# Moving the input sums, the first step tile's weights, the roots and the last chunk's first two tiles of a hybrid encoder layer

## The chip, the cores and the metric

The kernel runs on one core of a Trainium2 chip. The metric is the device time of one execution in microseconds (us). Each profile is one execution, recorded on the chip. The engines are PE (TensorE, matmuls), DVE (VectorE), ACT (ScalarE), POOL (GpSimd) and SP (SyncE, which here issues the loads).

## The reference

```python
def rmsnorm(x, g):
    return x * rsqrt(mean(x * x) + 1e-6) * g
def swiglu(x, wi, wo):
    a, b = split(x @ wi, 2)
    return (silu(a) * b) @ wo          # wi: 1024 x 5632, wo: 2816 x 1024
h = concatenate([meta, x])             # 16 + 512 positions, 1024 channels, fp32
h = h + 0.5 * rmsnorm(swiglu(rmsnorm(h, n[0]), ffn1_wi, ffn1_wo), n[1])
h = h +       rmsnorm(hybrid_mixer(rmsnorm(h, n[2]), ...), n[3])
h = h + 0.5 * rmsnorm(swiglu(rmsnorm(h, n[4]), ffn2_wi, ffn2_wo), n[5])
return h[16:]                          # the 512 positions of x
```

The mixer (a Fourier branch, a gated short convolution and a chunked gated DeltaNet) is not touched by the change.

## The kernel before

Everything is held transposed: channels on partitions (8 blocks of 128, index `k`), positions in the free dimension. `hT` is the residual, `x` the same with the gain of the norm but without its root: the product with `wi` is linear, so the root `rx` of each position is multiplied in afterwards (`scaled`, L531, and the `ev` products L643 and L646). Each fp32 matmul is made of three fp32r products, high by high, high by low and low by high, so that weights and inputs exist as pairs (`wh`, `wl`), (`x` twice), (`gh`, `gl`), (`h`, `l`). A split is a cast on ACT (L229 or L234) and a difference on DVE (L230 or L235). Weights land in `ws` or `wf` by loads on SP's queue and are split into a ring of four `wh` and `wl`.

The sections in order: the first FFN (`ffn`) over all 528 positions in halves of 264 columns; an `edge` (post norm, residual, pre norm and the first three weight units of the next section); the mixer; another `edge`, after which only the 512 real positions are left; the second FFN with matmuls of 512 columns; `finish`, which writes the output. PSUM has four banks `pb` and four `pd`.

Within an FFN there are 22 pairs (a, b) of 128 channels each of `wi`, in `CHUNKS` of 4, 4, 4, 4, 3 and 3. The first four pairs come from plain units: 8 blocks times 3 products into a bank. The other pairs use seven block products instead of eight (Strassen's way in Winograd's form): `seven` builds sums of blocks of the input (the input sums: `h`, `l`, L569 to L582, 128x1056 or 128x1024 elements each; the results are `X`), `one` to `seven` the products. The second product, with `wo`, makes 8 output tiles `m` from each chunk. `second` is one tile, `both` two tiles at once in plain order, `whole` one tile placed as a step between the products; the weights of two tiles come by `double`. For chunk 0 the tiles 0 to 3 come by `both`, and 4 to 7 as step tiles, whose split weights lie in `hx`, a tile in the same room as `hT` (tag "h"). `fetch` loads them. In that room lie the sums' inputs too, so that the room is free when the last sum has been read.

`xstat` sums squares for `rx`: ACT squares, DVE adds into `acc`, and then a step inside a unit (`side`, due at `XF` after the second edge) multiplies by `ones`, so that each partition gets the sum of each position, and `root` (ACT square root, L288, DVE reciprocal, L289) works on 128 partitions by 264 columns. `stat`, used for the post norms, instead sums into one column per 88 or 128 positions, takes the root there (positions on partitions, 88x3), and spreads it by matmuls of `ident` with the root broadcast and a copy (L285). The last chunk's tiles are left to `edge` or `finish` as a tail, in halves of the positions; `part` first copies `y` into the bank (L349), and the matmuls add onto it.

PE runs in the order of the code. The order on the other engines is set by the scheduler of the kernel language from dependencies and priorities: `high_priority(n)` moves what is inside ahead by n (`URGENT` 450, `AHEAD` 150, `AHEAD2` 200). Each engine then works strictly in that order.

Of the kernel before, what the change touches and what calls it, by code (L numbers as in the profile page):

```python
# [28 lines left out]
WARM = 9  # L29
AHEAD = 150  # L30
AHEAD2 = 200
XF = 9.0
URGENT = 450
CHUNKS = (range(0, 4), range(4, 8), range(8, 12), range(12, 16), range(16, 19), range(19, 22))
NU = max(len(c) for c in CHUNKS)
FIRST = 4
# [113 lines left out]
class K:  # L150
# [140 lines left out]
    def xstat(self, C, hT, rx, wait=XW, first=0):  # L291
        V, ACT = self.nc.vector, self.nc.scalar
        W = C.halves[0].stop - C.halves[0].start
        parts = []
        with self.tc.high_priority(first):
            for c in C.halves:
                acc = self.t(self.tp, "acc", [P, HN], F32, 2)[:, :W]
                ACT.activation(acc, hT[:, 0, c], AF.Square)
                for k in range(1, KD):
                    sq = self.t(self.tp, "sx", [P, HN], F32, 2)[:, :W]  # L300
                    ACT.activation(sq, hT[:, k, c], AF.Square)
                    V.tensor_tensor(acc, acc, sq, op=ALU.add)  # L302
                parts.append((acc, rx[:, c]))

        def gen():
            for acc, dst in parts:
                ps = self.dnp()[:, :W]
                self.T.matmul(ps, self.ones, acc, start=True, stop=True)
                self.root(ps, dst)
            yield 0.0  # L310
        self.side(gen(), wait)

# [3 lines left out]
        acc = [self.t(self.tp, "acc", [P, HN], F32, 2)[:, :W] for _ in range(2)]  # L316
        return y, acc

    def evict_y(self, ya, m, ps, gain=None, table=KD - 2, more=False):

        y, acc = ya
        ACT, V = self.nc.scalar, self.nc.vector
        for i, p in ps:
            w = acc[i].shape[1]
            if more:
                V.tensor_tensor(y[i][:, m, :w], y[i][:, m, :w], p, op=ALU.add)
                p = y[i][:, m, :w]
            elif gain is None:
                ACT.copy(y[i][:, m, :w], p)
            else:  # L330
                ACT.activation(y[i][:, m, :w], p, AF.Copy, scale=self.gains[:, gain, m:m + 1])
            if m == 0:
                ACT.activation(acc[i], p, AF.Square)
            else:
                sq = self.t(self.tp, "sy", [P, HN], F32, 1)[:, :w]
                ACT.activation(sq, p, AF.Square)  # L336
                V.tensor_tensor(acc[i], acc[i], sq, op=ALU.add)  # L337
            if more and gain is not None:
                ACT.activation(p, p, AF.Copy, scale=self.gains[:, gain, m:m + 1])
        if m == table:  # L340
            ACT.activation(self.junk, acc[0][:, :1], AF.Sqrt)

# [54 lines left out]
    def edge(self, C, hT, ya, gpost, gpre, tail, switch, nxt, keep=None):  # L397
        nc = self.nc
        V, ACT = nc.vector, nc.scalar
        W = C.halves[0].stop - C.halves[0].start  # L400
        r = self.t(self.tp, "r", [P, L])
        x = (self.xtile(), self.xtile())
        self.rx = rx = self.t(self.tp, "rx", [P, L])

        def step(i, k):
            c = C.halves[i]
            t = self.small()[:, :W]
            V.scalar_tensor_tensor(t, ya[0][i][:, k, :W], self.gains[:, gpost, k:k + 1], r[:, c],  # L408
                                   op0=ALU.mult, op1=ALU.mult)
            V.tensor_tensor(hT[:, k, c], hT[:, k, c], t, op=ALU.add)  # L410
            if keep is not None:
                nc.gpsimd.dma_start(keep[:, k, i * W:(i + 1) * W], hT[:, k, c])
            g = self.gains[:, gpre, k:k + 1]
            ACT.activation(x[0][:, k, c], hT[:, k, c], AF.Copy, scale=g)  # L414
            V.scalar_tensor_tensor(x[1][:, k, c], hT[:, k, c], g, x[0][:, k, c].bitcast(F32),  # L415
                                   op0=ALU.mult, op1=ALU.subtract)

        tiles, tx, tc, more = tail()
        for t in tiles:
            self.evict_y(ya, t[0], [(0, self.part(t, tx, tc[0], W, more and ya[0][0]))], table=tiles[0][0] - 1)  # L420
        post = [self.stat([(ya[1][i], r[:, C.halves[i]])]) for i in range(2)]

        def early():
            for _ in range(5):
                yield
            next(post[0])
            for _ in range(4):
                yield
            next(post[0], None)
            for k in range(3):  # L430
                step(0, k)
        e = early()
        for t in tiles:
            self.evict_y(ya, t[0], [(1, self.part(t, tx, tc[1], W, more and ya[0][1], lambda: next(e, None)))], table=-1)
        for k in range(3, KD):
            step(0, k)
        switch()
        ws = [self.load(a) for a in nxt]
        os = [self.outs(C), self.outs(C), self.outs(C, self.dnp)]
        LAG = 2  # L440
        for i in range(KD + LAG):
            if i in (SB0, SB1):
                next(post[1], None)
            for j in range(3):
                k = i - (LAG if j == 2 else 0)
                if 0 <= k < KD:
                    self.mm(os[j].half[:1], ws[j], x, k, k, k == 0, k == KD - 1)
        for k in range(KD):
            step(1, k)
            for j in range(3):  # L450
                self.mm(os[j].half[1:], ws[j], x, k, k, k == 0, k == KD - 1)
        self.xstat(C, hT, rx, *((XF, URGENT) if keep is not None else ()))
        return x, os

    def finish(self, hT, ya, tail, out):
# [20 lines left out]
        def early():  # L476
# [13 lines left out]
                yield  # L490
            for t in range(2):
                for f in range(2):
                    b = self.big()
                    for i in range(4):
                        T.transpose(b[:, i * P:(i + 1) * P],
                                    hT[:, 4 * f + i, cB.start + t * P:cB.start + (t + 1) * P], ident)
                        if i % 2:
                            yield
                    ACT.copy(hB[:, t, f * 512:(f + 1) * 512], b)
# [116 lines left out]
    def ffn(self, pre, wi, wo, C, hT, gpre, again, gain=None):  # L616
# [40 lines left out]
        with urgent():  # L657
# [1 line left out]
            silu(e[:, 0])  # L659
            self.scaled(e[:, 1], o2)  # L660
            pair(3, e[:, 0, u], e[:, 1, u])
        X, rest = self.seven(hT, C, gpre)
        rest()

        ya = self.start_y(C)
        later = []
# [1 line left out]
        def second(ci, m, w):  # L668

            n = len(CHUNKS[ci])  # L670
            final = ci == len(CHUNKS) - 1
            o = self.outs(C)

            def ks(r):
                for k in r:
                    self.mm(o.full, w, G[ci], (m % 2) * n + k, k, k == 0, k == n - 1)

            def evict():
                ps = [(i, p) for i, (p, _) in enumerate(o.half)]
                with urgent():  # L680
                    if final:
                        return self.evict_y(ya, m, ps, gain, more=True)
                    for i, p in ps:
                        y = ya[0][i][:, m, :W]
                        if ci:
                            V.tensor_tensor(y, y, p, op=ALU.add)  # L686
                        else:
                            ACT.copy(y, p)
            return ks, evict, n
# [13 lines left out]
            ks2([n - 1])  # L703
            evict2()

        for m in range(0, FIRST, 2):
            both(0, m)


# [6 lines left out]

        def fetch(i):
            if i < len(line) and i not in ready:
                ready[i] = double(*line[i], (room[i // 2 % 2], room[2 + i // 2 % 2]))

        def whole():
            nonlocal at
# [73 lines left out]
        for ci in range(1, len(CHUNKS)):  # L796
            n = len(CHUNKS[ci])
            for m in CHUNKS[ci]:
                if m == CHUNKS[ci].start + 1:
                    while at < limit:  # L800
                        whole()
                    acc = 0.0
                    if ci > 1:
                        limit += KD
                rate = (KD if ci > 1 else KD - FIRST) / (2.0 * n)
                nxt = one(m)
                five(nxt)
                slot(rate)
                if st:
                    seven(st)  # L810
                slot(rate)
                two(nxt)
                if st:
                    four(st)
                six(nxt)
                st = nxt
        slot(1.0)
        seven(st)
        while at < limit:
            whole()  # L820
        four(st)
        fin = len(CHUNKS) - 1
        hT = self.htile()
        for k in range(KD):
            nc.sync.dma_start(hT[:, k, u], again[:, k])
        both(fin, 0)

        def tail():
            n = len(CHUNKS[fin])
            ws = [double(fin, m) for m in range(2, KD, 2)]  # L830
            return [(m, [(ws[m // 2 - 1], (m % 2) * n + k, k) for k in range(n)]) for m in range(2, KD)], G[fin], C.halves, True
        return hT, ya, tail


# [756 lines left out]
```

## Time and profile before

| | us |
|---|---|
| median of three runs (lowest to highest) | 1308.08 (1306.58 to 1311.67) |
| the profiled execution, own time | 1309.39 |
| its span | 1307.6 |
| PE busy in the span | 1277.4 |
| first FFN to the first edge, from the span's start | 0 to 369 |
| edge 1 | 369 to 401 |
| mixer | 401 to 925 |
| edge 2 | 925 to 947 |
| second FFN | 947 to 1290 |
| finish | 1290 to 1307.6 |

A matmul's own duration holds its pipeline, so the distance from one start to the next is what it costs in a stream. A number in brackets behind a row of the timeline is how long the engine stood idle before it, and what it waited for. The granted clock in a window is the share of full speed at which PE was allowed to run.

### The profile page before, as it was taken

What the parts mean: (1) busy time and instruction counts of PE and PEld (TensorE: products, weight loads), DVE (VectorE), ACT (ScalarE), POOL (GpSimd) and SP (SyncE); (2) the same over time, 40 slices, a digit from 0 to 9 for tenths busy, and PEclk for the clock granted to TensorE, in tenths of its full rate; (3) what the DMA queues carried; (4) which work ended last, traced back from release to release, by engine and by line L of the source; (5) the groups of instructions that cost most, each with busy time, mean ns of one, the idle gap of its engine ahead of it and who ended that gap; (6) DMA issues with size and microseconds to landing.
All of it is one profiled execution on the core that took longest, in us unless ns stands there. A gap on an engine that the chain in (4) does not pass through costs nothing.

```text
span 1307.6 us, 22834 instructions
## 1 busy us (share of the span) xinstructions
PE 1277.4 (98%) x9001; PEld 1156.1 (88%) x9001; DVE 953.7 (73%) x1878; ACT 609.6 (47%) x1191; POOL 13.5 (1%) x28
## 2 busy tenths in 40 slices
PE   9999999999999999999999999999896999999997
PEld 9999999999989988779977777888875999999996
DVE  7968777766578889568788578463987677777655
ACT  7555444434275642444633444334555554444436
POOL 0000000000000000000000000000200000000000
PEclk9989999999999999999999999999998999999999
DMA  7233223222334222221221212234431332322213
GB/s 255 81 105 106 98 100 102 98 82 73 115 134 162 77 86 85 86 74 66 81 66 49 73 57 89 81 121 146 153 121 65 113 106 98 105 98 93 85 49 129
DMA packets 70205, 129.51 MB, mean 99 GB/s; under 512 B 15820, under 2 KB 24140, under 8 KB 70100
## 3 DMA queue, kind: packets, MB, share of 16 engines
q1 hardware_dynamic: 64244, 124.40, 28.2%
q10 hardware_dynamic: 5088, 1.57, 0.5%
q0 software_dynamic: 768, 2.10, 0.4%
q8 instruction: 70, 1.15, 0.4%
q14 instruction: 35, 0.29, 0.1%
HBM read 120.68 MB, written 7.37 MB: 98 GB/s over the span
## 4 chain that ended last, share of the span: by engine, by line
PE 88%; DVE 7%; ACT 3%; issue 1%; DVEq 0%; ACTq 0%
PE pb L143 55%; PE pd L143 32%; PE pd L147 1%; DVE s L408 1%; DVE x L415 1%; DVE acc L302 1%; DVE h L410 1%; DVE wl L235 1%; DVE wl L230 1%; DVE h L558 0%; ACT wh L229 0%; ACT sy L336 0%; DVE x L235 0%; DVE acc L337 0%; ACT pb L349 0%
## 5 line engine op out<-in xcount | busy, mean ns | idle before, releaser
L143 PE MATMUL pb<-x,wh 128*128 128x264 f32 (+3 forms) x1568 | 356.5, 331 | 5.4 <-ACT x L414 2.5
L143 PEld LDWEIGHTS pb<-x,wh 128*128 128x128 f32 x1568 | 247.7, 190 | 37.7 <-DVE x L415 5.1
L143 PE MATMUL pb<-x,wl 128*128 128x264 f32 (+3 forms) x784 | 219.9, 325 | 0.0
L143 PE MATMUL pb<-gh,h 128*128 128x264 f32 (+1 forms) x816 | 187.7, 327 | 10.6 <-ACT h L229 10.5
L229 ACT CAST wh<-ws 128x1024 fp32r<-128x1024 f32 (+2 forms) x114 | 107.3, 943 | 184.3 <-PE pb L143 145.7
L143 PE MATMUL pd<-x,wh 128*128 128x264 f32 (+2 forms) x1040 | 192.1, 285 | 0.0
L234 ACT CAST wh<-wf 128x1024 fp32r<-128x1024 f32 x108 | 113.4, 1050 | 161.9 <-PE pd L143 126.8
L235 DVE TENSOR_TENSOR wl<-wf,wh 128x1024 fp32r<-128x1024 f32 x108 | 132.0, 1222 | 42.8 <-ACT wh L234 42.7
L143 PEld LDWEIGHTS pd<-x,wh 128*128 128x128 f32 x1040 | 160.5, 189 | 2.0
L143 PEld LDWEIGHTS pb<-gh,h 128*128 128x128 f32 x816 | 131.2, 192 | 23.1 <-ACT h L229 10.9
L230 DVE TENSOR_TENSOR wl<-ws,wh 128x1024 fp32r<-128x1024 f32 (+2 forms) x114 | 123.7, 1086 | 30.7 <-ACT wh L229 30.3
L143 PEld LDWEIGHTS pb<-x,wl 128*128 128x128 f32 x784 | 133.9, 190 | 12.7 <-DVE wl L378 0.2
L143 PE MATMUL pd<-x,wl 128*128 128x264 f32 (+2 forms) x520 | 143.8, 284 | 0.0
L143 PE MATMUL pb<-gl,h 128*128 128x264 f32 (+1 forms) x408 | 110.8, 326 | 0.0
L143 PEld LDWEIGHTS pd<-x,wl 128*128 128x128 f32 x520 | 96.3, 188 | 0.3
L143 PE MATMUL pd<-h,wh 128*128 128x264 f32 (+1 forms) x294 | 82.2, 283 | 0.0
L143 PE MATMUL pd<-l,wh 128*128 128x264 f32 (+1 forms) x288 | 81.7, 284 | 0.0
L143 PE MATMUL pd<-h,wl 128*128 128x264 f32 (+1 forms) x288 | 81.4, 283 | 0.0
L143 PEld LDWEIGHTS pb<-gl,h 128*128 128x128 f32 x408 | 69.2, 192 | 4.9
L229 ACT CAST h<-ws 128x1024 fp32r<-128x1024 f32 (+1 forms) x36 | 35.9, 1003 | 65.1 <-PE pb L143 56.7
L686 DVE TENSOR_TENSOR y<-y,pb 128x264 f32<-128x264 f32 (+1 forms) x128 | 48.5, 420 | 20.4 <-PE pb L143 20.4
L143 PE MATMUL pb<-y,wh 128*128 128x512 f32 x192 | 61.7, 403 | 0.0
(318 smaller groups left out, 2313.1 us busy)
## 6 DMA issues: line engine op xcount, KB each, us to landing
wf<-in_wi SPq DMA_DIRECT2D x144, 256.0 KB, 2.6
ws<-in_wo SPq DMA_DIRECT2D x64, 256.0 KB, 2.8
ws<-in_win SPq DMA_DIRECT2D x32, 512.0 KB, 3.2
ws<-in_wg SPq DMA_DIRECT2D x24, 512.0 KB, 3.3
ws<-in_wi SPq DMA_DIRECT2D x13, 512.0 KB, 3.4
ws<-in_wo SPq DMA_DIRECT2D x32, 192.0 KB, 2.5
ws<-in_wout SPq DMA_DIRECT2D x8, 512.0 KB, 3.2
h<-in_xT SPq DMA_DIRECT2D x10, 264.0 KB, 3.2
```

The costliest lines, as they stand in the source:

```text
L143: return self.e.matmul(out, lhsT, rhs, **kw)
L147: return self.e.transpose(*a)
L229: nc.scalar.copy(h[:, :n], st[:, :n])
L230: nc.vector.tensor_tensor(l[:, :n], st[:, :n], h[:, :n].bitcast(F32), op=ALU.subtract)
L234: self.nc.scalar.copy(h, src)
L235: self.nc.vector.tensor_tensor(l, src, h.bitcast(F32), op=ALU.subtract)
L302: V.tensor_tensor(acc, acc, sq, op=ALU.add)
L408: V.scalar_tensor_tensor(t, ya[0][i][:, k, :W], self.gains[:, gpost, k:k + 1], r[:, c], op0=ALU.mult, op1=ALU.mult)
L410: V.tensor_tensor(hT[:, k, c], hT[:, k, c], t, op=ALU.add)
L415: V.scalar_tensor_tensor(x[1][:, k, c], hT[:, k, c], g, x[0][:, k, c].bitcast(F32), op0=ALU.mult, op1=ALU.subtract)
L686: V.tensor_tensor(y, y, p, op=ALU.add)
```

## The change

Four things are done.

1. `seven` (the input sums) is issued at priority `XAHEAD` = 150, ahead of the weight prefetch, and its second part `rest()` behind `both(0, 0)` instead of ahead of it.
2. `fetch(0)`, the weights of the first step tile pair (tiles 4 and 5 of chunk 0), goes to the ordinary ring of `wh` and `wl` instead of `hx`.
3. `xstat` takes its root by `stat`: positions on partitions, 88x6 or 128x4. `XF` goes from 9 to 6.
4. The last chunk has no `both(fin, 0)` any more: all eight of its tiles are the tail, by halves; evictions are issued at `URGENT`; the rate of step tiles in the last chunk and their last places are different. In `finish` the transposes of `hT` go to `pd` banks.

```diff
-XF = 9.0
+XF = 6.0
+XAHEAD = 150
...
         def gen():
-            for acc, dst in parts:
-                ps = self.dnp()[:, :W]
-                self.T.matmul(ps, self.ones, acc, start=True, stop=True)
-                self.root(ps, dst)
+            yield from self.stat(parts)
             yield 0.0
...
-    def evict_y(self, ya, m, ps, gain=None, table=KD - 2, more=False):
+    def evict_y(self, *a, **kw):
+        with self.tc.high_priority(URGENT):
+            self.leave_y(*a, **kw)
+
+    def leave_y(self, ya, m, ps, gain=None, table=KD - 2):
...
-            if more:
-                V.tensor_tensor(y[i][:, m, :w], y[i][:, m, :w], p, op=ALU.add)
-                p = y[i][:, m, :w]
-            elif gain is None:
+            if gain is None:
...
-            self.evict_y(ya, t[0], [(0, self.part(t, tx, tc[0], W, more and ya[0][0]))], table=tiles[0][0] - 1)
+            self.evict_y(ya, t[0], [(0, self.part(t, tx, tc[0], W, more and ya[0][0]))], table=KD - 2)
...
-                    b = self.big()
+                    b = self.dnp()
...
-        X, rest = self.seven(hT, C, gpre)
-        rest()
+        with self.tc.high_priority(XAHEAD):
+            X, rest = self.seven(hT, C, gpre)
...
-        for m in range(0, FIRST, 2):
+        both(0, 0)
+        with self.tc.high_priority(XAHEAD):
+            rest()
+        for m in range(2, FIRST, 2):
             both(0, m)
...
-                ready[i] = double(*line[i], (room[i // 2 % 2], room[2 + i // 2 % 2]))
+                ready[i] = double(*line[i], (room[i // 2 % 2], room[2 + i // 2 % 2]) if i else None)
...
+                if ci == len(CHUNKS) - 1:
+                    rate = (KD - 4) / (2.0 * n)
...
-        slot(1.0)
+        whole()
         seven(st)
+        whole()
+        four(st)
         while at < limit:
             whole()
-        four(st)
...
-        both(fin, 0)
...
-            ws = [double(fin, m) for m in range(2, KD, 2)]
-            return [(m, [(ws[m // 2 - 1], (m % 2) * n + k, k) for k in range(n)]) for m in range(2, KD)], G[fin], C.halves, True
+            ws = [double(fin, m) for m in range(0, KD, 2)]
+            return [(m, [(ws[m // 2], (m % 2) * n + k, k) for k in range(n)]) for m in range(KD)], G[fin], C.halves, True
```

What the change does to the order of instructions is seen at three places.

DVE in the first FFN, before, from the root of the pre norm on (`RECIPROCAL`). L531 twice is the evacuation of one unit from two banks `pb`, L558 a scaling of `hT` for the input sums:

```order
L289 RECIPROCAL rx_90<-rx_90 128x264 x2
L230 TENSOR_TENSOR wl_642<-ws_640,wh_641 128x1024
L643 TENSOR_TENSOR ev_375<-ev_375,rx_90 128x528 x2
L646 TENSOR_TENSOR ev_376<-ev_376,rx_90 128x528
L230 TENSOR_TENSOR wl_741<-ws_739,wh_740 128x1024
L531 TENSOR_TENSOR ev_376<-pb_389,rx_90 128x264
L630 TENSOR_TENSOR ev_375<-ev_375 128x528
L531 TENSOR_TENSOR ev_376<-pb_390,rx_90 128x264
L558 SCALAR_TENSOR_TENSOR h_87<-h_87,gains_77,rx_90 128x528
```

The same place after the change, from the row behind the reciprocal on (now `rt` of 88x6), where the lines are three lower (L528, L555, L640, L643) or one higher (L231, L236, L290):

```order
L603 TENSOR_TENSOR wf_1097<-wf_1097,wf_1100 128x512
L231 TENSOR_TENSOR wl_654<-ws_652,wh_653 128x1024
L528 TENSOR_TENSOR ev_376<-pb_389,rx_90 128x264
L555 SCALAR_TENSOR_TENSOR h_87<-h_87,gains_77,rx_90 128x528 x6
L231 TENSOR_TENSOR wl_743<-ws_741,wh_742 128x1024
L555 SCALAR_TENSOR_TENSOR h_87<-h_87,gains_77,rx_90 128x528 x2
L236 TENSOR_TENSOR l_78_725<-h_87,h_77_724 128x1056
L640 TENSOR_TENSOR ev_375<-ev_375,rx_90 128x528
L236 TENSOR_TENSOR l_78_725<-h_87,h_77_724 128x1056
L640 TENSOR_TENSOR ev_375<-ev_375,rx_90 128x528
L643 TENSOR_TENSOR ev_376<-ev_376,rx_90 128x528
L528 TENSOR_TENSOR ev_376<-pb_390,rx_90 128x264
```

The evacuation of the second half (`pb_390`) now stands behind all eight scalings and two splits of the input sums, and behind the three products of `ev`. (In the names, `l` and `h` are the split sums, `ev` a unit's results.)

DVE in the second FFN, before, the end of the input sums (L572 to L582) and the first step tile's low weights (`h_10676` from `ws`):

```order
L572 SCALAR_TENSOR_TENSOR ev_10577<-ev_10577,h_9643 128x4x256
L574 SCALAR_TENSOR_TENSOR h_9643<-h_9643,ev_10577 128x4x256
L235 TENSOR_TENSOR wl_10857<-wf_10843,wh_10856 128x1024
L235 TENSOR_TENSOR x_10589<-ev_10577,x_10588 128x4x256
L235 TENSOR_TENSOR x_10589<-h_9643,x_10588 128x4x256 x2
L582 SCALAR_TENSOR_TENSOR x_10589<-h_9643,x_10588 128x4x256
L608 TENSOR_TENSOR wf_10970<-wf_10969,wf_10971 128x512
L610 TENSOR_TENSOR wf_10971<-wf_10972,wf_10971 128x512
L230 TENSOR_TENSOR h_10676<-ws_10681,h_10676 128x1024
L230 TENSOR_TENSOR h_10676<-ws_10760,h_10676 128x1024
```

After the change, from the split of the gated product of pair 1 (`gl_10521` from `ev_10404`) to that of pair 2 (from `ev_10531`) and the start of the sums' second part; `wl_10723` are the low weights of the first step tile:

```order
L231 TENSOR_TENSOR wl_10723<-ws_10721,wh_10722 128x1024
L236 TENSOR_TENSOR gl_10521<-ev_10404,gh_10520 128x512
L528 TENSOR_TENSOR ev_10531<-pb_10445,rx_9876 128x512
L528 TENSOR_TENSOR ev_10538<-pb_10545,rx_9876 128x512
L528 TENSOR_TENSOR ev_10531<-pd_10492,rx_9876 128x512
L627 TENSOR_TENSOR ev_10531<-ev_10531 128x512
L528 TENSOR_TENSOR ev_10538<-pb_10576,rx_9876 128x512
L236 TENSOR_TENSOR wl_10738<-wf_10728,wh_10737 128x1024
L627 TENSOR_TENSOR ev_10538<-ev_10538 128x512
L236 TENSOR_TENSOR gl_10521<-ev_10531,gh_10520 128x512
L566 TENSOR_TENSOR ev_10617<-h_9674 128x4x256
L236 TENSOR_TENSOR gl_10521<-ev_10538,gh_10520 128x512
```

The first step tile's weights moved from behind the last sum to ahead of the splits of pairs 1 to 3.

PE at the root ahead of the second FFN, before:

```order
L143 MATMUL pb_10413<-x_9843,wl_10409 128x512
L143 MATMUL pd_10432<-acc_10325,ones_78 128x256
L143 MATMUL pd_10436<-acc_10348,ones_78 128x256
L143 MATMUL pb_10413<-x_9843,wh_10408 128x512
L143 MATMUL pb_10413<-x_9844,wh_10408 128x512
```

And after the change:

```order
L144 MATMUL pb_10445<-x_9874,wl_10441 128x512
L144 MATMUL pd_10452<-ones_78,acc_10357 128x1 x2
L144 MATMUL pd_10452<-ones_78,acc_10380 128x1 x2
L144 MATMUL pb_10445<-x_9874,wh_10440 128x512
L144 MATMUL pb_10445<-x_9875,wh_10440 128x512
```

Two wide matmuls became four of one column, and after nine matmuls of the plain unit (`pb`) come four of 128 columns, `ident` by the root `rt`, which these rows no longer show.

More of the change, by code (lines that the diff above doesn't have):

```diff
@@ L337, in evict_y @@
                 V.tensor_tensor(acc[i], acc[i], sq, op=ALU.add)
-            if more and gain is not None:
-                ACT.activation(p, p, AF.Copy, scale=self.gains[:, gain, m:m + 1])
         if m == table:
@@ L670, in second @@
             n = len(CHUNKS[ci])
-            final = ci == len(CHUNKS) - 1
             o = self.outs(C)
@@ L680, in evict @@
                 with urgent():
-                    if final:
-                        return self.evict_y(ya, m, ps, gain, more=True)
                     for i, p in ps:
```

## The prediction

> **What bounds the kernel now.** I read the page first, then the waits of PE, then the granted clock over the stretches with the longest waits, and last the timeline there. The page (engine shares; the chain that ended last) says:
>
> ```profile
> PE 1277.4 (98%) x9001; PEld 1156.1 (88%) x9001; DVE 953.7 (73%) x1878; ACT 609.6 (47%) x1191; POOL 13.5 (1%) x28
> PE 88%; DVE 7%; ACT 3%; issue 1%; DVEq 0%; ACTq 0%
> ```
>
> PE sets the end: in the chain (second row) it has 88%. Work on DVE, ACT or SP is free unless PE waits for it, so only three things are worth microseconds: matmuls added or removed, PE's waits, and half clock. The waits of PE (total, times, longest) begin with:
>
> ```profile
> PE pb L143 <- ACT h L229: 10.5, 2, 8.2
> ```
>
> These two waits are the first step tile of each FFN (tile 4): its weights are cast into `hx`, which lies in the room of `hT`, and so after the last input sum. The windows (PE busy, ..., granted clock, DMA) show what follows such a wait:
>
> ```profile
> 72.00:78.00 6.00, 5.74 (x24) 5.43 (x25) 5.01 (x6) 2.09 (x3) 0.00 (x0) 0.50 0.53 159
> 376.00:379.00 3.00, 1.59 (x7) 1.03 (x7) 2.86 (x9) 3.00 (x8) 0.04 (x1) 1.00 0.89 315
> 379.00:382.50 3.50, 3.18 (x15) 3.14 (x15) 3.50 (x10) 2.28 (x7) 0.00 (x0) 0.51 0.73 279
> 997.00:1007.00 10.00, 5.30 (x12) 3.71 (x13) 7.60 (x9) 1.99 (x2) 0.00 (x0) 0.50 0.34 109
> ```
>
> Half clock follows idle PE: 3.5 us of it after edge 1's stretch that is half idle (376 to 379), 6 us after the first FFN's wait of 2.3 us, 10 us around the second's of 8.2. Half of the busy part is lost, so one stretch like edge 1's costs 1.7, two cost 3.4. The page "TensorE: Matmul & The Clock Gate" of the Trainium skill (Part 1, "What's actually happening") says that the clock halves after at least one idle window of about 3.4 us. By that rule a wait of 2.3 us would not halve it; this trace does not agree, and I go by the rows.
>
> **Second FFN, the gain.** PE and what it waited for, from the timeline:
>
> ```profile
> 989.29 0.28 PE L143 MATMUL pd<-h,wl 128*128 128x256 f32 x1
> 990.27 0.39 PE L143 MATMUL pb<-h,wh 128*128 128x256 f32 x1 [0.70 <-ACT h L234]
> 991.87 0.39 PE L143 MATMUL pb<-l,wh 128*128 128x256 f32 x1 [1.21 <-DVE l L235]
> 993.17 0.28 PE L143 MATMUL pb<-h,wl 128*128 128x256 f32 x1
> 999.27 1.21 DVE L582 SCALAR_TENSOR_TENSOR x<-h,x 128x1024 fp32r<-128x1024 f32 x1
> 1000.56 1.99 ACT L229 CAST h<-ws 128x1024 fp32r<-128x1024 f32 x2 [3.94 <-issue]
> 1001.66 0.79 PE L143 MATMUL pb<-gh,h 128*128 128x512 f32 x1 [8.21 <-ACT h L229]
> 1006.92 0.50 PE L143 MATMUL pb<-gh,h 128*128 128x512 f32 x1
> 958.32 0.39 PE L143 MATMUL pb<-x,wl 128*128 128x512 f32 x1
> 958.55 0.62 PE L143 MATMUL pb<-x,wh 128*128 128x512 f32 x2
> ```
>
> A 512-column matmul takes 0.23 us at full clock (958.32 to 958.55). The losses, as start to start less one matmul: 0.9 at 990.27, 1.5 at 991.87, 8.4 at 1001.66 (993.17 before it); and twelve matmuls from 1001.66 to one pace past 1006.92, 5.5 us at half clock where 2.8 would do: 2.8. Together 13.5. The change takes them all away: tile 4 reads an ordinary `wh` cast before the sums, and the sums come earlier. The tile pair 6, 7 does use `hx`, and its cast waits for the last sum. By the paces below the sums end 11 steps of 1.14 and one of 0.60 after `gl` of pair 2 (979.8), at 993, and the cast by 996. PE wants it after 42 matmuls of 512 columns that are left of `both(0, 0)` and `both(0, 2)`, 24 of tiles 4 and 5, and 48 of 256 columns: 9.7 + 5.5 + 5.6, at 1000.6. So 4.6 us are in hand. The `in_wo` loads of tile 4 stand two to four loads earlier on SP, ahead of `wf` loads; an SP issue waits in that queue, but these weights are cast long before PE needs them. POOL's queue is as before.
>
> What is late next is `gl`, the low part of a pair's gated product, since eight row scalings and two `l` now stand ahead of it on DVE. The paces there:
>
> ```profile
> 958.13 3.36 DVE L289 RECIPROCAL rx<-rx 128x256 f32<-128x256 f32 x2 [0.85 <-ACT rx L288]
> 964.29 0.68 DVE L531 TENSOR_TENSOR ev<-pb,rx 128x512 f32<-128x512 f32 x1
> 964.89 0.74 DVE L558 SCALAR_TENSOR_TENSOR h<-h,gains,rx 128x512 f32<-128x512 f32 x1
> 973.23 2.73 DVE L558 SCALAR_TENSOR_TENSOR h<-h,gains,rx 128x512 f32<-128x512 f32 x4
> 976.12 0.69 DVE L531 TENSOR_TENSOR ev<-pb,rx 128x512 f32<-128x512 f32 x1 [0.16 <-PE pb L143]
> 997.00 2.35 DVE L235 TENSOR_TENSOR x<-h,x 128x1024 fp32r<-128x1024 f32 x2
> ```
>
> Start to start: 0.60 (964.29 to 964.89), 0.67 (2.73 for four), 1.14 (2.35 for two). The root is full at about 958.2 (an estimate: the sums at 957.0, two casts and a small reciprocal) where the 3.36 us held it until 961.5. From there to `gl` of pair 2 the new order has 8 scalings, 7 wide splits and 15 of 0.60: 5.4 + 8.0 + 9.0 = 22.4, so 980.6; one split may run before the root, so 979.5 to 980.6, and I take 979.8. PE's last plain unit ended about 976.1 (row 976.12 waits for it); with 1.1 of new root work and 0.7 to 1.4 of pairs 0 and 1, PE wants it at 977.9 to 978.6. A wait of 1 to 2.5; I take 2.0, and 0.8 for an even chance of one stretch of half clock. Net here: 13.5 + 0.3 (a wait for `gl` at 980.8) - 2.8 = **-11.0**. Ends: -7.9 (a wait of 2.5 and two stretches) and -12.8 (a wait of 1 alone).
>
> **Roots.** Old: two matmuls of 264 columns with `ones` moving, in two passes each. New: one-column sums, then matmuls of `ident` with the root broadcast, as the post statistics do already:
>
> ```profile
> 30.69 1.05 PE L143 MATMUL pd<-acc,ones 128*128 128x264 f32 x4
> 31.39 0.84 PE L143 MATMUL pb<-x,wh 128*128 128x264 f32 x4
> 31.85 3.46 DVE L289 RECIPROCAL rx<-rx 128x264 f32<-128x264 f32 x2 [1.43 <-ACT rx L288]
> 368.88 0.63 PE L143 MATMUL pd<-ones,acc 128*88 128x1 f32 x6
> 369.37 0.37 PE L143 MATMUL pb<-gh,wh 128*128 128x264 f32 x1
> 371.08 0.90 PE L143 MATMUL pd<-ident,rt 88*128 88x88 f32 x6
> 371.77 0.37 PE L143 MATMUL pb<-gh,wh 128*128 128x264 f32 x1
> 1291.58 0.69 PE L143 MATMUL pd<-ident,rt 128*128 128x128 f32 x4
> 1292.03 0.37 PE L143 MATMUL pb<-gh,wh 128*128 128x256 f32 x1
> ```
>
> Old: 0.70 and 0.2 of slow start: 0.9. New, 264 columns twice: 2 x (0.49 + 0.69) = 2.4, with slow starts 3.0 at most; I take 2.5, so +1.6 each before the first FFN and the mixer. New, 256 columns: 2 x (0.45 + 0.45) and 0.2: 2.0, so +1.1. Together **+4.3** (3.9 to 5.6). DVE is freed of 3.3 us at each, which counts only where PE waits for DVE. At the mixer it does not, so there the +1.6 is paid for nothing. The chain in between (root on ACT, reciprocal, copies) is covered by 10 to 19 matmuls, 2.3 us; uncovered it would cost that.
>
> **First FFN.** Before, the sums were late and PE waited 2.3 us; now PE waits sooner, for a bank. Between the two halves of the second evacuation (L531 twice) DVE had one product; now it has eight scalings, the `l`s, three scalings of `ev` and a `wl`. Rows:
>
> ```profile
> 39.29 0.42 DVE L531 TENSOR_TENSOR ev<-pb,rx 128x264 f32<-128x264 f32 x1
> 40.34 0.42 DVE L531 TENSOR_TENSOR ev<-pb,rx 128x264 f32<-128x264 f32 x1
> 42.58 0.65 PE L143 MATMUL pb<-x,wh 128*128 128x264 f32 x4
> 69.67 0.28 PE L143 MATMUL pb<-h,wl 128*128 128x264 f32 x1
> 72.25 0.81 PE L143 MATMUL pb<-gh,h 128*128 128x264 f32 x2 [2.30 <-ACT h L229]
> ```
>
> The unit of pair 3 starts at 42.58 into that bank, 44.1 with the new root. Root full at 35.7 (35.3 before: an estimate as above); then 0.35 + 8 x 0.67 + 3 x 1.14 + 3 x 0.60, and 0.35 for the second half itself: 11.3, so the bank is free at 47.0. Wait 2.9; half clock after it 2.0, by the first FFN's old wait of 2.3 and edge 1's (0 to 3.4); and `gl` of pair 3, which now stands behind the sums, 0 to 1.9: I take 1.2. New loss 6.1. Old loss: 2.5 (69.67 to 72.25 less one pace) and 2.9 (half of the 5.74 busy at 0.50): 5.4. Net **+0.7** (-5.4 if DVE is quicker than PE here, +2.8).
>
> **Edges and end.** Tiles 0 and 1 of the last chunk move from `both(fin, 0)` into the tail, whose sums start from a preloaded bank: the matmuls are the same. Rows of what PE loses there:
>
> ```profile
> 369.26 1.28 ACT L288 ACT_TABLE_LOAD   x1
> 377.00 0.39 PE L143 MATMUL pb<-x,wh 128*128 128x264 f32 x1 [1.22 <-ACT x L414]
> 1283.06 0.39 PE L143 MATMUL pb<-gh,wh 128*128 128x256 f32 x1 [0.57 <-ACT pb L349]
> ```
>
> ACT begins its tail work earlier, with four more preloads and copies to do. Of edge 1's loss, 1.2 and the 1.7 of half clock at 379, I count 1.0 as gained (-2.9, or +2 where the table load now stands ahead of an eviction that PE waits for). At the end the 0.57 goes and 0.3 comes back, for two evictions more: -0.3 (+-1). Two tiles of the second FFN in halves: 0.1, for 36 matmuls of 256 columns where 18 of 512 were.
>
> **Sum** against the profiled run's 1309.4 us (span 1307.6): -11.0 + 4.3 + 0.7 - 1.0 - 0.3 + 0.1 = -7.2, so 1302.2; the median of the runs shown (1308.1) is 1.3 lower, so **1300.9**.
>
> **Rivals.** (A) As summed, 1297.5 to 1304: 0.43. (B) The new waits eat it: in the second FFN the wait for `gl` is 2.5 and two stretches of half clock follow (+3.1), in the first FFN two stretches and the full 1.9 (+2.1, 1.4 and 0.7): 1306.1, no change that a measurement of this kernel can tell (under 0.5%, 6.5 us). For it: at 72 and at 997 a wait was followed by more than one stretch; against it: both new waits are shorter than the 8.2. 0.26. (C) Slower: DVE's strict order. The `l` splits wait for casts that stand on ACT behind a weight cast, which waits until PE frees a slot; if DVE stands there x us in each FFN, the bank and `gl` are x later and PE with them, and the half clock is two stretches each time (+4.0 over A). 1300.9 + 4.0 + 2x ends over 1314.6 from x = 5 on. Against it: ACT is 47% busy and a weight cast takes 1.0. 0.10. (D) The bank wait of the first FFN hides, since DVE or the casts let it through sooner: 4.9 less than A, 1296.0; DVE's 3.3 us saved there speak for it, 2.9 of computed wait against it. 0.16. (E) Half clock needs PE idle for a whole stretch, so the new waits cost only themselves: 2.8 less than A, 1298.1; the row at 72 speaks against it. 0.05. This is the rule of the Trainium skill's clock page named above.
>
> **How the numbers follow.** Faster by over 0.5% (below 1301.5): 0.26 of A's 0.43, D and E: 0.47. Within 0.5%: the rest of A, and B: 0.43. Slower: 0.10. The range goes from 1294 (D with the second FFN's better end) to 1309 (B with the upper bounds of the roots and half of edge 1's), which leaves out C and a little at the lower end.
>
> **What would show it.** Right: no `pb <- ACT h L229` wait of microseconds, none of 0.5 clock near 1000; a PE wait for a bank freed by DVE near 44 to 47 and one for `gl` near 978. Wrong: a wait of the second `hx` tile pair in either FFN, a wait at the roots, or more than 3 us at the last tiles' evictions on ACT.

## The result and the profile after

The changed kernel takes 1300.62 us (median of six runs) against 1308.47 of the kernel before: ratio 0.9936, 95% interval 0.9921 to 0.9951. The forecast was 1300.9. One of the six took 1539.57 us at a granted clock of 0.75; it counts in the median but not in the ratio, and the other five have a median of 1299.97. The profiled execution took 1301.27 us (span 1299.4), 8.1 less than before's 1309.39.

The page of the changed kernel, engine shares and the chain that ended last:

```profile
PE 1275.8 (98%) x9071; PEld 1157.2 (89%) x9071; DVE 942.5 (73%) x1867; ACT 615.9 (47%) x1208; POOL 13.4 (1%) x28
PE 88%; DVE 7%; ACT 3%; issue 1%; DMA 1%; SPq 0%; DVEq 0%; ACTq 0%
```

PE still sets the end. Its waits (total, times, longest):

```profile
PE pb L144 <- DVE x L412: 3.6, 9, 0.8
PE pb L144 <- DVE ev L528: 2.8, 1, 2.8
PE pb L144 <- DVE gl L236: 1.7, 2, 1.2
...
PE pb L144 <- ACT mh L235: 1.1, 1, 1.1
...
PE pb L144 <- ACT gh L235: 1.0, 1, 1.0
```

The row that headed the list before, 10.5 us for the cast into `hx`, is gone. In its place stand the bank (L528), `gl` and `gh`, and one that the prediction did not have, `mh` (near the mixer's end). The waits in the timeline, with the DVE instruction that frees the bank:

```profile
44.41 0.28 PE L144 MATMUL pb<-x,wh 128*128 128x264 f32 x1
47.44 0.81 PE L144 MATMUL pb<-x,wh 128*128 128x264 f32 x2 [2.75 <-DVE ev L528]
46.96 0.43 DVE L528 TENSOR_TENSOR ev<-pb,rx 128x264 f32<-128x264 f32 x1
66.78 0.51 PE L144 MATMUL pb<-gl,wh 128*128 128x264 f32 x2 [1.22 <-DVE gl L236]
983.14 0.50 PE L144 MATMUL pb<-gh,wh 128*128 128x512 f32 x1 [0.98 <-ACT gh L235]
984.14 0.51 PE L144 MATMUL pb<-gl,wh 128*128 128x512 f32 x1 [0.50 <-DVE gl L236]
997.00 0.39 PE L144 MATMUL pb<-gh,wh 128*128 128x512 f32 x1
998.35 2.00 ACT L230 CAST h<-ws 128x1024 fp32r<-128x1024 f32 x2
1005.43 0.39 PE L144 MATMUL pb<-gh,h 128*128 128x512 f32 x1
```

At 997.00 the first step tile of the second FFN starts with no wait; the cast into `hx` (998.35) now serves tiles 6 and 7, which PE reaches only at 1005.43. The windows of half clock (PE busy, ..., granted clock, DMA) are two of 3.4 us, behind the bank wait and at edge 1; around 984 there is none:

```profile
47.00:50.50 3.50, 3.06 (x14) 3.06 (x15) 3.42 (x7) 2.19 (x4) 0.00 (x0) 0.51 0.24 63
381.70:385.00 3.30, 3.13 (x14) 3.14 (x15) 2.88 (x8) 0.87 (x2) 0.00 (x0) 0.50 0.91 366
981.00:985.00 4.00, 2.51 (x10) 1.50 (x10) 3.97 (x6) 2.71 (x4) 0.00 (x0) 1.00 0.18 65
```

Where the time went is read from the same matmul in both traces. The table gives its start in us, and what the stretch up to it gained or lost beside what was forecast for it:

| mark on PE | before | after | this stretch | forecast |
|---|---|---|---|---|
| first `pd<-x,w4h` of the first FFN | 97.29 | 99.15 | +1.86 | +2.3 (root 1.6, waits 0.7) |
| first matmul of the mixer (128x258) | 405.73 | 406.50 | -1.09 | -1.0 |
| first transpose `ident,t` of 16 positions | 422.52 | 424.55 | +1.26 | +1.6 (root) |
| last `mh,wh` of 512 columns (mixer's end) | 904.16 | 908.09 | +1.90 | 0 |
| first `pd<-x,wh` of the second FFN | 959.24 | 963.90 | +0.73 | +1.1 (root) |
| first `pd<-x,w4h` of the second FFN | 1025.58 | 1018.09 | -12.15 | -10.9 |
| last `ones,sy` | 1300.91 | 1292.88 | -0.54 | -0.3 |
| sum | | | -8.03 | -7.2 |

### The profile page after: what moved, and what is told of

It is laid out like the page before. It is cut to its first block, busy times and chain, and to the rows that moved or that the text cites. A ratio compares the mean times of both kernels' runs of the same rounds, so it can differ in the third digit from the quotient of the medians.

```text
span 1299.4 us, 22964 instructions
## 1 busy us (share of the span) xinstructions
PE 1275.8 (98%) x9071; PEld 1157.2 (89%) x9071; DVE 942.5 (73%) x1867; ACT 615.9 (47%) x1208; POOL 13.4 (1%) x28
## 4 chain that ended last, share of the span: by engine, by line
PE 88%; DVE 7%; ACT 3%; issue 1%; DMA 1%; SPq 0%; DVEq 0%; ACTq 0%
PE pb L144 54%; PE pd L144 32%; DVE wl L231 1%; PE pd L148 1%; DVE acc L303 1%; DVE s L405 1%; ACT pb L346 1%; DVE h L407 1%; DVE x L412 0%; DMA ws<-in_wout 0%; ACT wh L230 0%; DVE l L236 0%; ACT sy L335 0%; DVE acc L336 0%; DMA h<-in_xT 0%
## 5 line engine op out<-in xcount | busy, mean ns | idle before, releaser
L144 PE MATMUL pb<-gh,h 128*128 128x264 f32 (+1 forms) x768 | 172.8, 321 | 0.0
L236 DVE TENSOR_TENSOR wl<-wf,wh 128x1024 fp32r<-128x1024 f32 x108 | 132.0, 1223 | 39.4 <-ACT wh L235 39.0
L231 DVE TENSOR_TENSOR wl<-ws,wh 128x1024 fp32r<-128x1024 f32 (+2 forms) x116 | 126.2, 1090 | 33.1 <-ACT wh L230 32.7
L144 PEld LDWEIGHTS pb<-gh,h 128*128 128x128 f32 x768 | 120.9, 188 | 10.4
L144 PE MATMUL pb<-gl,h 128*128 128x264 f32 (+1 forms) x384 | 102.6, 321 | 0.0
L144 PEld LDWEIGHTS pb<-gl,h 128*128 128x128 f32 x384 | 63.6, 188 | 4.6
```

Source lines behind the costliest of these rows:

```text
L144: return self.e.matmul(out, lhsT, rhs, **kw)
L231: nc.vector.tensor_tensor(l[:, :n], st[:, :n], h[:, :n].bitcast(F32), op=ALU.subtract)
L236: self.nc.vector.tensor_tensor(l, src, h.bitcast(F32), op=ALU.subtract)
```

## The experiments

All times are medians; each kernel has its own ratio to the kernel before, timed beside it. What a part costs or brings against the changed kernel is worked out from the ratios.

| kernel | weights of tiles 4, 5 | early sums | new roots | new tail | us | ratio (95% interval) |
|---|---|---|---|---|---|---|
| before | hx | no | no | no | 1308.5 | 1 |
| changed | ring | yes | all | yes | 1300.6 | 0.9936 (0.9921 to 0.9951) |
| w_alone | ring | no | no | no | 1293.5 | 0.9887 (0.9871 to 0.9904) |
| hx_again | hx | yes | all | yes | 1305.9 | 0.9977 (0.9968 to 0.9987) |
| sums_late | ring | no | all | yes | 1293.2 | 0.9880 (0.9865 to 0.9895) |
| roots_old | ring | yes | no | yes | 1306.3 | 0.9981 (0.9969 to 0.9992) |
| evac_first | ring | yes, behind two evacuations | all | yes | 1300.0 | 0.9932 (0.9910 to 0.9955) |
| tail_w | ring | no | no | yes | 1293.3 | 0.9881 (0.9866 to 0.9895) |
| root_one | ring | no | second FFN | yes | 1290.3 | 0.9858 (0.9843 to 0.9873) |
| sums_second | ring | second FFN | second FFN | yes | 1293.2 | 0.9876 (0.9860 to 0.9893) |
| root_one_old_tail | ring | no | second FFN | no | 1291.5 | 0.9864 (0.9843 to 0.9884) |
| roots_both_edges | ring | no | mixer and second FFN | yes | 1294.1 | 0.9875 (0.9856 to 0.9895) |

**The weights alone (w_alone).** On the kernel before:

```diff
-                ready[i] = double(*line[i], (room[i // 2 % 2], room[2 + i // 2 % 2]))
+                ready[i] = double(*line[i], (room[i // 2 % 2], room[2 + i // 2 % 2]) if i else None)
```

> The kernel before with one part of the change alone: the weights of step tiles 4 and 5 go to the ordinary ring, sums, roots and tail stay as they were. Theory 1 (the weights' place is the cause of the long waits, and the early sums are not needed for it): the waits of 8.2 and 2.3 us for the cast into hx and the half clock behind them go (8.4 + 2.8 in the second FFN, 5.4 in the first), the waits for sums (0.9 + 1.5 in the second FFN) stay, and tiles 6 and 7, still in hx, wait 1 to 2 us: 1308.5 - 14 = 1294.5, between 1291 and 1299, so faster than the changed kernel (1300.6). Theory 2 (the late sums are the cause, and a wait only moves to the next product or to tiles 6 and 7): 1303 to 1307.

1293.5: theory 1, one us better than its middle. This one line brings 14.8 us by its ratio, where the whole change brings 8.4. What is left of waits in its second FFN:

```profile
990.97 0.38 PE L143 MATMUL pd<-x,wh 128*128 128x256 f32 x1 [1.06 <-DVE x L235]
995.50 0.51 PE L143 MATMUL pb<-gh,h 128*128 128x512 f32 x1 [0.17 <-ACT h L229]
997.25 0.73 PE L143 MATMUL pb<-gh,h 128*128 128x512 f32 x2 [1.01 <-DVE h L230]
```

The wait for the late sums is 1.06, and tiles 6 and 7 wait 0.17 and 1.01. In the first FFN, behind the root, no wait is above 0.3 us. At the marks of the table above it gains 5.5 us in the first FFN and 10.6 in the second.

**The weights back in hx (hx_again).** The same line the other way round, on the changed kernel.

> The changed kernel with the weights of step tiles 4 and 5 back in hx; early sums, roots and tail as changed. Theory 1 (the place of the weights): in the second FFN the last sum ends at 997.5 and the cast and split follow at 998.4 to 1001, while PE wants tile 4 at 997.0: a wait of some 3 us, with or without half clock of 1.7 to 3.4; in the first FFN the sums end at 71.4 and PE wants tile 4 at 77.2: none. 1303.5 to 1307, at 1305. Theory 2 (the early sums alone bring the gain): no wait, 1300.6 as the changed kernel. Theory 3 (the place is the whole gain): 1312.

1305.9, theory 1. The wait at the first step tile is there again, if short (timeline):

```profile
1003.39 0.51 PE L144 MATMUL pb<-gh,h 128*128 128x512 f32 x1 [2.24 <-ACT h L230]
1004.84 1.22 PE L144 MATMUL pb<-gh,h 128*128 128x512 f32 x2 [0.57 <-DVE h L231]
```

Behind it the profiled execution has 6.8 us of half clock. This execution is the slowest of ten (1311.4); it also waited 1.19 us for its first weights at 12 us, with 3.4 us of half clock behind that, ahead of anything that the line moves.

```profile
1003.90:1010.70 6.80, 6.23 (x18) 4.90 (x18) 3.91 (x5) 1.65 (x4) 0.00 (x0) 0.50 0.69 218
```

**The sums late (sums_late).** On the changed kernel:

```diff
-        with self.tc.high_priority(XAHEAD):
-            X, rest = self.seven(hT, C, gpre)
+        X, rest = self.seven(hT, C, gpre)
+        rest()
...
-        both(0, 0)
-        with self.tc.high_priority(XAHEAD):
-            rest()
-        for m in range(2, FIRST, 2):
+        for m in range(0, FIRST, 2):
             both(0, m)
```

> The changed kernel with the input sums at the old priority and both parts of them ahead of the first tiles in the code; weights, roots and tail as changed. Theory 1 (the early sums cost more than they bring): in the first FFN the bank wait of 2.75 us, 1.7 of half clock and 1.2 for gl go; in the second FFN 1.5 for gl goes and 0 to 4 comes back as waits for sums and for tiles 6 and 7. 1300.6 - 7 + 0 to 4: 1294 to 1298, at 1296. Theory 2 (the early sums are needed now that the weights are early): the waits of 0.9 and 1.5 for sums come back, tiles 6 and 7 wait 3 us and half clock follows: 1303 to 1306.

1293.2, below the low end of theory 1. The early sums cost 7.3 us. In its second FFN, from 955 to 1010, one wait is left, and in the first none of note; there is no half clock in the whole span before the end:

```profile
PE pb L144 <- DVE gl L236: 0.3, 1, 0.3
```

Neither the sums nor tiles 6 and 7 were waited for: the 0 to 4 that I had kept for them is 0. The first FFN's mark is 5.8 us earlier than in the changed kernel, the second FFN 1.5 us shorter, 7.3 together; edge 1 is 1.4 shorter, since no half clock came there.

**The old roots (roots_old).** The changed kernel with the loop over `parts` (matmul with `ones`, `root`) back in `xstat`, and `XF = 9.0`.

> The changed kernel with the old root of the pre norms (wide matmuls with ones, square root and reciprocal on 128 partitions, XF 9); weights, sums and tail as changed. Theory 1 (the new roots pay for their matmuls by an earlier root): PE is 1.3 + 1.3 + 1.0 = 3.5 us shorter, but rx in the second FFN is full 2.8 us later against PE and gl of pair 2 with it, so that its wait grows from 1.5 to 5.3 with half clock of 1.7 to 3.4 behind it; in the first FFN the bank wait grows from 2.75 to some 4.5. Net +3 to +6: 1303.5 to 1306.5. Theory 2 (the new roots only cost): 1297.1.

1306.3, theory 1: with early sums the new roots are worth 5.9 us net. Its waits, first FFN and second:

```profile
PE pb L144 <- DVE ev L531: 5.5, 1, 5.5
PE pb L144 <- ACT gh L235: 5.8, 2, 3.4
```

Both waits follow the root on DVE: 5.5 where 2.75 was, and 5.8 where 1.5 was.

**The evacuations first (evac_first).** On the changed kernel:

```diff
-        self.scaled(b1, o)
+        with urgent():
+            self.scaled(b1, o)
...
-        self.scaled(e[:, 0], o2)
+        with urgent():
+            self.scaled(e[:, 0], o2)
         silu(e[:, 0])
-        self.scaled(e[:, 1], o3)
+        with urgent():
+            self.scaled(e[:, 1], o3)
```

> The changed kernel with one thing more: the evacuations of the units of pairs 1 and 2 (scaled) are issued at URGENT, so that both halves of a bank pair leave PSUM before the eight scalings of the input sums; order of the code, sums, weights, roots and tail as changed. Theory 1 (the new wait of PE in the first FFN is a bank held by DVE's order): the wait of 2.75 us at 47.4 goes, with the half clock of 1.7 behind it, while the wait for gl of pair 3 (1.2) stays or grows by up to 1: 1300.6 - 4 = 1296.6 (1295.5 to 1298). Theory 2 (DVE is simply too full there): PE waits as long for the next thing, the gl of the pairs or the sums: 1299 to 1301.

The runs lie at 1297 and 1298 and at 1302 and 1303, so the median of 1300.0, in theory 2's range and not in theory 1's, decides little. The trace decides on the place: the wait of 2.75 and the half clock behind it are gone, and two shorter ones came later:

```profile
52.38 0.36 PE L144 MATMUL pb<-x,wh 128*128 128x264 f32 x1 [1.22 <-DVE ev L528]
52.96 0.64 PE L144 MATMUL pb<-x,wh 128*128 128x264 f32 x3 [0.23 <-DVE ev L528]
```

The first FFN's mark is 3.4 us earlier than in the changed kernel (95.75 for 99.15). The profiled execution (1302.3) gives it back at two places. At edge 1 the half clock lasts 10.2 us for the changed kernel's 3.4 (2.7 us by the marks). In the second FFN, where the edit puts the same evacuations ahead too, `gl` comes 0.9 later against PE: the wait of 0.50 is 1.36, and half clock follows where the changed kernel had none (2.4 us by the marks):

```profile
377.30:387.50 10.20, 9.57 (x43) 9.28 (x44) 7.02 (x18) 3.55 (x9) 0.00 (x0) 0.50 0.46 159
984.90:988.30 3.40, 3.40 (x10) 2.62 (x9) 3.37 (x4) 2.04 (x2) 0.00 (x0) 0.50 0.00 0
```

```profile
983.61 0.50 PE L144 MATMUL pb<-gl,wh 128*128 128x512 f32 x1 [1.36 <-DVE gl L236]
```

So the bank's wait is shown to come from DVE's order. That the evacuations moved ahead made `gl` later is likely, but was not tried apart.

**Weights and tail (tail_w)**, sums and roots as before the change: sums_late and roots_old together.

> The kernel before with two parts: weights of tiles 4 and 5 in the ordinary ring, and the new tail; sums late and all three roots old, XF 9. From the kernel with the weights alone (1293.5) the tail takes 2.5 us at edge 1 (no half clock there) and 0.5 at the end. Theory 1 (the parts add): 1290.5 (1289 to 1292), below the kernel with the new roots too (1293.2), since these cost 1.6 in the first FFN, 1.3 and a wait of 1.7 at the mixer, and win 2 in the second FFN. Theory 2 (the new roots are needed for the early tail or in the second FFN): 1293 or more.

1293.3: neither better than the weights alone nor than with the new roots, so the parts do not add as I read them from the marks. The edge gains 1.3 by the marks, the end 0.5; the profiled start is 1.3 slower (a wait of 1.04 us at 11 us for the first weights, which differs from run to run), and the medians show no difference.

**The new root at the second FFN only (root_one).** As sums_late, with

```diff
-            yield from self.stat(parts)
-            yield 0.0
+            if C.joined:
+                yield from self.stat(parts)
+                yield 0.0
+                return
+            for acc, dst in parts:
+                ps = self.dnp()[:, :W]
+                self.T.matmul(ps, self.ones, acc, start=True, stop=True)
+                self.root(ps, dst)
+            yield 0.0
```

> As the one with weights and tail, but with the new root at the second FFN only (XF 6), the old at the two places with 528 positions; sums late. Theory 1: of the kernel with all new roots (1293.2) the first FFN gives back 1.6, the mixer 1.3 of matmuls and the wait of 1.7 near its end, which stood in all three kernels with a new root ahead of the mixer and in none without; the second FFN keeps its gain of 2.2: 1288.5 (1287 to 1290), the fastest so far. Theory 2 (the wait near the mixer's end has nothing to do with that root): 1290.3.

1290.3, the fastest of all and faster than both kernels. This is theory 2's number, though the savings of theory 1 stand in the trace: against sums_late 1.3 in the first FFN and 1.3 and 1.1 in the mixer, of which edge 1 takes 1.7 back, with 3.4 us of half clock that sums_late did not have. By the medians the old root at these two places saves 2.9. Against tail_w the root at the second FFN is worth 3.0 by the medians: tail_w's waits of 1.06 and 1.02 us are gone, for 0.9 of matmuls. By the marks it is 2.1; the rest is tail_w's wait for its first weights.

**The sums early in the second FFN only (sums_second).** root_one, with the priority and the later `rest()` if `C.joined`.

> As the one with the new root at the second FFN only, but with the input sums early in the second FFN alone (priority 150, second part behind both(0, 0)). Theory 1 (early sums only make gh and gl of the pairs late: waits of 1.0 and 0.5 us, as in the changed kernel): 1.5 slower than without, 1290. Theory 2 (with the first FFN left out, early sums help the second): 1287 or less.

1293.2: 3.0 slower, theory 1 with half clock added (timeline, then window):

```profile
973.70 0.50 PE L144 MATMUL pb<-gh,wh 128*128 128x512 f32 x1 [0.98 <-ACT gh L235]
974.98 0.50 PE L144 MATMUL pb<-gl,wh 128*128 128x512 f32 x1 [0.78 <-DVE gl L236]
```

```profile
975.60:978.90 3.30, 3.30 (x9) 2.61 (x8) 3.30 (x4) 1.99 (x2) 0.00 (x0) 0.50 0.02 8
```

**The old tail (root_one_old_tail).** root_one with the tail of the kernel before.

> The fastest version so far (weights of tiles 4 and 5 in the ring, new root at the second FFN alone, late sums, new tail: 1290.3) with the old tail: tiles 0 and 1 of the last chunk by both(fin, 0) and the adds of banks at the edge. Theory 1 (the new tail is worth what the marks in the traces say, 1.3 at edge 1 and 0.5 at the end): 1292.1 (1291.3 to 1293). Theory 2 (the new tail is worth nothing, as the equal medians of 1293.5 without and 1293.3 with it suggest): 1290.3.

1291.5 (1291.0 to 1293.7), with a ratio whose interval covers that of root_one. The new tail is worth about 1 us or nothing; this does not settle it.

**The new root ahead of the mixer too (roots_both_edges).** root_one with `if C.joined or edge`, where `edge` is true for the calls from `edge`.

> The fastest version so far (1290.3) with the new root ahead of the mixer as well (and the old one only at the start). Theory 1 (that root costs PE 1.3 us of matmuls and, because the program is longer by some instructions, a code load falls into a load of in_wout near the mixer's end, which makes PE wait 1 us and more): 1290.3 + 1.3 + 1.0 to 1.8 = 1293 (1292.4 to 1293.5). Theory 2 (the collision depends on the new root at the start as well): 1291.6.

1294.1, but not by theory 1's way: no code load fell into that load here, and the stretch at the mixer's end is 0.4 longer and not 1.9. The root itself costs 1.3 by the marks. The rest of the profiled run's loss against root_one is 2.4 at edge 1 (10.1 us of half clock, where root_one had 3.4), 1.1 in the first FFN (a wait for the first weights) and 0.6 at the end. So in this trace the new root ahead of the mixer did not by itself bring the collision, as theory 2 said; theory 2's time of 1291.6 was not met either.

## Why the prediction was right

**The gain of the second FFN** was computed as 13.5 lost before, less 2.8 of new waits, 0.3 of which stood there before. Measured: -12.15 for -10.9 with the split tiles. The old losses went entirely (no wait at 997.00): in sums_late, where one wait of 0.3 is left, the stretch gains 13.65. Against that the changed kernel loses 1.5, where 2.5 was computed. Of the new wait, the `gl` of pair 2, I took 2.0 and 0.8 of half clock. As the prediction counts losses, from start to start less a matmul, it was 1.9 (0.98 and 0.50 of idle time), and the half clock did not come. So the 1.3 that the stretch came out better is mostly this half clock, a chance that fell well. The rows behind the wait:

```profile
980.38 0.69 DVE L627 TENSOR_TENSOR ev<-ev 128x512 f32<-128x512 f32 x1
980.57 1.05 ACT L235 CAST wh<-wf 128x1024 fp32r<-128x1024 f32 x1 [0.17 <-PE pb L144]
981.53 1.05 ACT L578 ACTIVATE x<-h 128x1024 fp32r<-128x1024 f32 x1
982.49 0.60 ACT L235 CAST gh<-ev 128x512 fp32r<-128x512 f32 x1
983.40 0.69 DVE L236 TENSOR_TENSOR gl<-ev,gh 128x512 fp32r<-128x512 f32 x1
```

The product of pair 2 was ready at 981.07, but its cast `gh` stood on ACT behind a weight cast and a piece of the sums (L578), and PE first waited for that. The prediction had left ACT's order out of its sum; only (C) named it. It did not set the end of the wait here: `gl` came at its place in DVE's order, at 984.09. The spare time of tiles 6 and 7 held: 4.6 computed; the cast of their first part ended at some 999.4, and PE came at 1005.43, 6.0 later.

**The first FFN's bank** was computed row by row along DVE's order: free at 47.0, PE there at 44.1, wait 2.9. Measured: PE there at 44.5, the bank free at 47.4, wait 2.75. `gl` of pair 3: 1.2 for 1.22. Half clock: 1.7 for 2.0. This is the surest part, and evac_first shows the place, since two evacuations moved ahead take that wait away.

**The roots** cost 1.26 at the mixer where 1.6 was counted, and 0.73 at the second FFN (edge 2's 0.2 gain in it) for 1.1. The rows of the changed kernel:

```profile
31.09 1.03 PE L144 MATMUL pd<-ones,acc 128*88 128x1 f32 x12
31.98 0.73 PE L144 MATMUL pb<-x,wh 128*128 128x264 f32 x4
34.27 1.47 PE L144 MATMUL pd<-ident,rt 88*128 88x88 f32 x12
35.53 0.73 PE L144 MATMUL pb<-x,wh 128*128 128x264 f32 x4
```

0.89 and 1.26, 2.15 in all, 1.25 more than the 0.9 of the old root: twelve matmuls in a row cost less than twice six. The three roots together cost some 3.4 of matmuls (1.25, 1.26 and 0.9) where 4.3 was counted.

**Edge 1** came out at -1.09 for -1.0, but not in the way that the forecast gave. It counted on losing part of the wait of 1.22 and of the half clock. The wait of 1.22 is gone, but three others stand at the same kind of matmul, and the half clock is as long as before, 3.4 us:

```profile
379.34 0.39 PE L144 MATMUL pb<-x,wh 128*128 128x264 f32 x1 [0.70 <-DVE x L412]
380.99 0.39 PE L144 MATMUL pb<-x,wh 128*128 128x264 f32 x1 [0.78 <-ACT x L411]
381.87 0.59 PE L144 MATMUL pb<-x,wh 128*128 128x264 f32 x1 [0.49 <-DVE x L412]
```

So here the size was right, and the reason for it is not shown.

**What it missed** are 1.9 us at the mixer's end, where I had counted nothing: the sum came out near because this and the smaller waits in the second FFN offset each other. In the changed kernel a load of `in_wout`, issued at 869.70, was late; ACT, DVE and PE follow it, and PE loses 1.8 there from start to start:

```profile
875.51 1.05 ACT L230 CAST wh<-ws 128x1024 fp32r<-128x1024 f32 x1 [2.33 <-DMA ws<-in_wout]
885.19 0.50 PE L144 MATMUL pb<-mh,wh 128*128 128x512 f32 x1 [1.06 <-ACT mh L235]
```

**What the sum could not show** is which part paid. It forecast -11.0 from weights and sums together; the runs separate them. The weights' place is worth 14.8 alone (ratio 0.9887), and 5.4 with the rest of the change (0.9977 to 0.9936), since early sums free `hx` sooner too; the early sums, which I took as part of the cure, cost 7.3. So the total was right while its parts were not known: the largest gain came from one part, and another part took half of it back. The 4.3 of the roots is wrong as a pure cost, too: I wrote that DVE is freed of 3.3 us which counts only where PE waits for DVE, but put no number on it. In the second FFN it counts for 2 to 3 net with late sums, at the other two places it is a loss of 2.9 together.

Of the rivals, (D), that the bank wait hides, fell by the row at 47.44. (B) asked for two stretches of half clock in each FFN, and there was one in all. (C) asked for DVE 5 us late in each FFN; the bank of the first FFN was free at 47.4 for 47.0 computed. (E), a whole idle window before the clock halves, fell again: 2.75 us of wait were followed by 0.51 of full speed for 3.5 us, and in sums_second even two waits of 0.98 and 0.78 by 0.50. The rule stands in the Trainium skill, "TensorE: Matmul & The Clock Gate", Part 1; no run here bears it out as the least idle time that halves the clock.

## What to carry to other kernels

Where PE waits for a cast that waits for a buffer's last reader, give that one cast another buffer before reordering the work that makes the reader late: here the buffer was one line and some 15 us, while the reordering put other instructions, a bank's release and the splits of the gated products, behind the moved work. An evacuation that frees a bank belongs ahead of work on the same engine that is waited for later, but look at what it then stands ahead of (in evac_first one wait went, and another became longer). Walk the engine's new order with the trace's paces, and such a wait comes out to some tenths. A cheaper operation on a side engine is worth taking only at the place where the main engine waits for it.

## What the runs showed of the hardware that was not expected

A code load (a packet on the queue that the page calls instruction) may hold up a data load. In the four kernels with all new roots (changed, hx_again, sums_late, evac_first) a row of the instruction queue falls in the 4 us behind the issue of the second `in_wout` load, here for the changed kernel (packets, MB, share):

```profile
q1 hardware_dynamic: 137, 0.50, 37.7%
q8 instruction: 1, 0.02, 1.5%
```

In these four the fourth load, which has to wait until the second's buffer is read, starts 3.4 to 4.3 us behind the third, where it is 2.3 in the kernel before, and in three of them PE waits 0.9 to 1.2 us for `mh`. In the other eight kernels no such packet falls there. That the packet delays the load fits all twelve traces but was not tried by itself.

The half clock at edge 1 varies between executions of nearly the same work: none in the profiles of sums_late and roots_old, 3.4 us in the changed kernel's and root_one's, 10.2 and 10.1 in those of evac_first and roots_both_edges. The waits there are alike (about 0.7, 0.8 to 0.9 and 0.2 to 0.5 us in a row). The spread of some 5 us between runs of evac_first has this as its likely cause: the mean granted clock was 0.993 and 0.994 in its two runs of 1302 and 1303, 0.997 and 0.998 in the other two, and the share that is missing, times the span, is some 8.5 us and 3.2, an estimate whose difference, 5.3, is that of the times. Where the half clock fell is seen only in the profiled run.

The traces show a part of what decides it. The stretches last 3.4, 6.8 or 10.2 us, multiples of one length (3.413 us in the traces' record of the clock). In the changed kernel PE was busy for 1.64 us of the one length ahead of the stretch at edge 1; it was 1.87 in root_one, 1.93 in evac_first and 1.99 in roots_both_edges. In sums_late, with the length laid out back from the half clock at its end, the same waits fall into two lengths, and both are busier:

```profile
378.20:381.60 3.40, 1.64 (x8) 1.03 (x7) 3.40 (x10) 3.31 (x9) 0.00 (x0) 1.00 0.87 231
370.50:373.90 3.40, 2.40 (x16) 1.78 (x15) 3.40 (x8) 3.29 (x8) 0.20 (x2) 1.00 0.79 216
373.90:377.30 3.40, 2.13 (x16) 1.72 (x15) 3.40 (x10) 2.34 (x6) 0.00 (x0) 1.00 0.90 319
```

So it fits these traces that the place of the waits against such steps counts, and not their sum alone; nothing was run to test it. It is not a threshold: in roots_old two lengths of 1.55 and 1.93 (975.6 to 982.4) were followed by none. Why one stretch lasts 3.4 us and another 10.2 is open.
